# Second block's output projections: fp32 operands as they are, or split into two parts and multiplied in three passes

## The chip, the cores and the metric

The kernel runs on one core of a Trainium2 chip. Its time is the device time of one execution in microseconds (us), and a kernel's figure is the median over several executions. The engines named here are TensorE (PE, matrix products), VectorE (DVE), ScalarE (ACT), GpSimd (POOL) and SyncE (SP, which issues the loads). Each engine runs its instructions in the order in which they stand in its queue; semaphores make one engine wait for another.

## The reference, cut to what matters

The first part is a block of two layers (short convolution and retention) on 512 tokens of width 1024. Its result goes through a second block:

```
xn = rms_norm(h, norm1_g)
proj = xn @ w_in                      # queries, gates, values ...
o_hgrn = hgrn2_mixer(...)             # 4 heads of 128
o_gla  = gla_mixer(...)               # 4 heads of 128
mixed = concatenate([o_hgrn, o_gla])  # 512 tokens x 1024
h = h + mixed @ w_out                 # the output projections of the title
hn = rms_norm(h, norm2_g)
h = h + peer_ffn(hn, ...)             # top 16 of product keys, 128*128 experts
return rms_norm(h, norm_f_g)
```

All of it is in float32. `peer_ffn` computes queries `hn @ w_q`, compares them with sub-keys, and takes the top 16 of 8 heads twice. The kernel computes three of the four groups of 128 tokens densely over all experts, with a gate matrix made from the picks, and gathers the experts' rows for the fourth.

## The kernel before

A tensor is held with its 1024 columns on the partitions, in 8 pieces of 128, and its tokens along the free axis. The second block handles the tokens in two halves of 256. A weight matrix comes as tiles of 128 x 1024 through one list of tasks (`Weights`): SP loads the tiles in the list's order, and each task is then given its tiles.

A task can take its weights in two ways. With `direct=True` it gets the loaded tile, and `proj` (line 874) issues one fp32 matmul for each of the 8 pieces; the chip's profile shows each of them as two records. Otherwise ACT copies the tile to a tile `hi` of a shorter format (line 143), DVE subtracts it from the original and writes the rest to `lo` (line 151), and `proj` issues three matmuls for each piece: w hi by x hi, w hi by x lo, w lo by x hi (`PASSES`). The other operand has to be split as well, by `split_act` (lines 200 to 205) or `split_steps`: an ACT copy and a DVE subtraction. Splits of weights stand two tiles ahead of the task that uses them, with a raised priority.

The order of the second block is a list of words:

```
PLAN = "FQ00 P3 S00 P4 FQ01 S01 !N1 KG V0 G0 FQ10 S02 V1 S10 M00 FQ11 S11 G1 S12 M01 M10 O0 P8 M11 N0 Q00 O1 Q01 N1 P5 Q1"
```

The first digit is the half. S are the mixers' scores (line 1004 on PE, with DVE and ACT in between). M makes the mixer's outputs (`outs`, line 1124 on PE), their norm r (ACT, lines 214 to 1134), the normalised tiles `on` (DVE, line 1137), and transposes and gates them (`flips`, lines 1149 and 1151). O is the output projection: 8 tasks `wout_task` for each half, called at line 1541. Their input m is the gated tile itself. N is the norm behind it (x or hn), and Q the queries of the top 16 (`wq_task`), from half 0's split x (line 887) and half 1's fp32 hn (line 883). Keys are compared at line 1188. The selection of the top 16 (`top_k`, lines 1314 to 1385, mostly on DVE) and the gate matrices (`oh` on DVE, lines 1438 and 1445; products on PE, line 1453; copies on ACT, line 1462) are generators in the background: a few steps of them are issued at each tick, that is during and after each weight task. The expert products follow at lines 1718 and 1721 (up) and 1765 (down).

A scheduler that estimates durations orders the instructions on every engine when the program is built, with priorities from the order of issue. So an added instruction can move others.

Of the kernel before, what the change touches and what calls it, by code (L numbers as in the profile page):

```python
# [8 lines left out]
F32R = mybir.dt.float32r  # L9
# [14 lines left out]
HALF = 256  # L24
# [145 lines left out]
def tile_kernel(ctx: ExitStack, tc: tile.TileContext, ins, out):  # L170
# [15 lines left out]
    def ps_tile(role="a"):  # L186
        tag, n = psum["roles"].get(role, psum["roles"]["a"])
        return psum["pool"].tile([128, 512], F32, tag=tag, bufs=n, name="ps")
# [12 lines left out]
    def split_act(hl, src):  # L201

        x = nc.scalar.activation(hl[0], src, AF.Copy)
        nc.vector.tensor_tensor(out=hl[1], in0=src, in1=hl[0].bitcast(F32), op=OP.subtract)  # L204
        return x
# [87 lines left out]
    g = blocks.enter_context(tc.tile_pool(name="g", bufs=1, reuse_waits="tile"))  # L293
    NT = 10

    def slot(name, n=T, dt=F32):
        tag, bufs = SLOTS.get(name, ("g", NG))
        return g.tile([128, n], dt, tag=tag, bufs=bufs, name=name)
# [4 lines left out]
    def do(f, *a):  # L303
        W.add(lambda: f(*a))
# [530 lines left out]
    halves = []  # L835

    def second_block():
            def col(j):
                return cols2[:, j:j + 1]
# [30 lines left out]
            def pair(x):  # L870

                return x.rearrange("p (c t) -> p c t", c=2)
# [17 lines left out]
            def half(s):  # L890
                t0 = NM + HALF * s
                d = {}
# [250 lines left out]
                def flips(grp, i):  # L1143
                    p = ps_tile("o")
                    for hh in range(2):
                        h = 2 * i + hh
                        for t in range(2):
                            o = hh * HALF + t * 128
                            nc.tensor.transpose(p[:, o:o + 128], d["on", grp, t][:, h * 128:(h + 1) * 128], ident)
                    g = d.pop(("gate", grp, i))  # L1150
                    nc.vector.scalar_tensor_tensor(out=g, in0=p, scalar=col(E_HG + grp), in1=g, op0=OP.mult,
                                                   op1=OP.mult)
                    for hh in range(2):
                        d["m", 4 * grp + 2 * i + hh] = pair(g)[:, hh]
                    if i == 1:
                        for t in range(2):
                            d.pop(("on", grp, t))
# [60 lines left out]
            def pair_both(which, c):  # L1218

                def f(w):  # L1220
                    ds = [h["d"] for h in halves]
                    if c == 0:
                        for d in ds:
                            d["ps"] = ps_tile("ab")
                    proj(w, [(d["ps"][:, c * HALF:(c + 1) * HALF], d["x"]) for d in ds])
                    if c == 1:
                        for d in ds:
                            d[which, 2] = slot(which, 2 * HALF)
                            nc.scalar.activation(d[which, 2], d["ps"], AF.Copy, scale=0.125 if which == "q" else 1.0)
                return f  # L1230
# [35 lines left out]
            def v_task(grp, kp):  # L1266
                def f(w):
                    if kp == 0:
                        vps[:] = [(h["d"], t, ps_tile("v")) for h in halves for t in range(2)]
                    w = [x.rearrange("p (k c) -> p k c", c=512) for x in w]  # L1270
                    for kk in range(2):
                        k = 2 * kp + kk
                        for d, t, p in vps:
                            for n, (xi, wi) in enumerate(PASSES):
                                nc.tensor.matmul(p, d["x"][k][:, xi, t * 128:(t + 1) * 128], w[wi][:, kk, :],
                                                 start=(k == 0 and n == 0), stop=(k == KD - 1 and n == 2))
                    if kp == 3:
                        for j, (d, t, p) in enumerate(vps):
                            v = slot("v", 512)
                            nc.scalar.activation(v, p, AF.Copy)  # L1280
                            d["v", grp, t] = v
                            if j < 2:
                                first["v", grp, t] = v
                        vps.clear()
                return f

            def gate_task(grp, c):
                def f(w):
                    ds = [h["d"] for h in halves]
                    if c % 2 == 0:  # L1290
                        for d in ds:
                            d["ps"] = ps_tile("ab")
                    o = c % 2 * HALF
                    proj(w, [(d["ps"][:, o:o + HALF], d["x"]) for d in ds])
                    if c % 2:
                        for d in ds:
                            d["gate", grp, c // 2] = (slot if d is ds[1] else tb)("gate", 2 * HALF)
                            nc.scalar.activation(d["gate", grp, c // 2], d["ps"], AF.Silu)
                    if grp == 1 and c == 3:
                        for d in ds:  # L1300
                            d.pop("x")
                return f
# [180 lines left out]
            def add(f, direct=False, at=None):  # L1483
                W.add(f, n[0] if at is None else at, direct=direct)
                n[0] += at is None
# [4 lines left out]
            def back(s, f, *a, **k):  # L1490
                do(lambda: W.later(halves[s][f](*a), **k))
# [4 lines left out]
            def mixed(s, grp):  # L1496
                if s == 1:
                    for h in range(4):
                        call(s, "across", 4 * grp + h)
                        do(W.pump, 1)  # L1500
                call(s, "outs", grp)
                do(W.pump, 2)
                for i in range(2):
                    call(s, "flips", grp, i)
                    do(W.pump, 2)

            def retrieve(s, at, part=None):
                if part != 1:
                    call(s, "load_keys")
                for c in (range(16), range(QCUT), range(QCUT, 16))[0 if part is None else part + 1]:  # L1510
                    add(halves[s]["wq_task"](c), direct=s == 1, at=at + c)
                if part != 0:
                    call(s, "keys", 15)

            def step(name, *a):
                a = [int(x) for x in a]
                s = a[0] if a else 0
                if name == "FQ":
                    g2 = a[1]
                    for k, which in enumerate("fq"):  # L1520
                        for c in range(2):
                            add(halves[s]["pair_task"](which, 2 * g2 + c), direct=s == 0, at=N0 + 4 * g2 + 2 * k + c)
                elif name == "S":
                    back(s, "scores", a[1], name=f"S{s}{a[1]}")
                elif name == "KG":
                    for k, which in enumerate("kq"):
                        for c in range(2):
                            add(pair_both(which, c), at=N0 + 8 + 2 * k + c)
                    do(low_gate)
                elif name == "V":  # L1530
                    for kp in range(4):
                        add(v_task(s, kp), at=N0 + 12 + 8 * s + kp)
                elif name == "G":
                    for c in range(4):
                        add(gate_task(s, c), at=N0 + 16 + 8 * s + c)
                elif name == "M":
                    do(W.flush, *(f"S{s}{g}" for g in ((0, 1), (2,))[a[1]]))
                    mixed(*a)
                elif name == "O":
                    for m in range(KD):  # L1540
                        add(halves[s]["wout_task"](m), direct=True, at=N0 + 28 + m)
                elif name == "N":
                    back(s, "norm2", name="norm2", first=True)
                    do(W.flush, "norm2")
                elif name == "Q":
                    retrieve(s, N0 + 36, *a[1:])

            N0 = 256
# [3 lines left out]
            for word in PLAN.split():  # L1552
                if word[0] == "!":
                    do(W.flush, *word[1:].split(","))
                elif word[0] == "P":
                    pace(PACE[int(word[1:])])
                else:
                    name = word.rstrip("01234")
                    step(name, *word[len(name):])
# [401 lines left out]
```

## Time and profile before

| | us |
|---|---|
| median of 3 runs | 3293.77 (3293.57 to 3298.85) |
| the profiled execution | 3293.37 |
| its span on the core | 3291.6 |
| PE busy | 3250.3 (99%) |
| DVE busy | 2036.7 (62%) |
| ACT busy | 1302.2 (40%) |

The span goes from the first instruction to the last. A busy PE is one with a matmul in its pipe: a record's duration is longer than the distance to the next one, so the distance between starts is the price of one. The second block's output projections of half 0 run from 1885 to 1943 us, among the mixers' last steps, those of half 1 from 2010 to 2038, among the top-16 work. A row of the timeline merges neighbouring instructions of one kind.

### The profile page before, as it was taken

How to read it: one execution, taken by the hardware profiler on the slowest of the kernel's cores; microseconds unless marked ns; L12 is line 12 of the kernel's file. 1: busy time of each engine (PE TensorE's matmuls, PEld its weight loads, DVE VectorE, ACT ScalarE, POOL GpSimd, SP SyncE). 2: the span in 40 equal slices, each digit the busy share in tenths (PEclk: the TensorE clock that was granted, in tenths of full speed). 3: DMA queues.
4: the chain of work that ended last, by engine and by line, in shares of the span. 5: the costliest groups of instructions: out<-in, count | busy, mean ns of one | idle time of the engine just before them, and what ended most of it. 6: DMA issues, size and time to landing. Idle time of an engine off the chain costs nothing. (4 is left out here: it accounts for less than half of the span.)

```text
span 3291.6 us, 51099 instructions
## 1 busy us (share of the span) xinstructions
PE 3250.3 (99%) x21063; PEld 2974.2 (90%) x21063; DVE 2036.7 (62%) x4019; ACT 1302.2 (40%) x2388; POOL 186.3 (6%) x132
## 2 busy tenths in 40 slices
PE   8999999999999999999999999999999999999999
PEld 7999999999889999999998988766789999999998
DVE  6545554433744555443465659998898888888443
ACT  5343242323534324232455533356443333333333
POOL 0000000000000000000000000000132222222000
PEclk9999999999999999999999999999999999999999
DMA  6222222222422222222232123346899988998442
GB/s 216 75 86 88 77 78 90 90 90 103 176 75 99 87 84 78 90 90 100 106 129 90 52 91 140 129 181 239 305 373 346 345 333 314 351 356 325 143 147 95
DMA packets 129961, 532.04 MB, mean 162 GB/s; under 512 B 9136, under 2 KB 60992, under 8 KB 73280
## 3 DMA queue, kind: packets, MB, share of 16 engines
q1 hardware_dynamic: 103520, 368.19, 31.2%
q0 software_dynamic: 18432, 134.23, 10.6%
q10 hardware_dynamic: 7776, 26.37, 2.0%
q8 instruction: 165, 2.70, 0.3%
q14 instruction: 68, 0.56, 0.0%
HBM read 501.48 MB, written 27.26 MB: 161 GB/s over the span
## 5 line engine op out<-in xcount | busy, mean ns | idle before, releaser
L143 ACT ACTIVATE hi<-raw 128x1024 fp32r<-128x1024 f32 x532 | 563.4, 1060 | 1404.1 <-PE ps L386 626.7
L151 DVE TENSOR_TENSOR lo<-raw,hi 128x1024 fp32r<-128x1024 f32 x532 | 650.6, 1224 | 753.3 <-ACT hi L143 748.4
L386 PE MATMUL ps<-xnh,hi 128*128 128x256 f32 (+1 forms) x2464 | 513.7, 283 | 0.0
L386 PE MATMUL ps<-xnl,hi 128*128 128x256 f32 (+1 forms) x2464 | 513.5, 283 | 0.0
L386 PE MATMUL ps<-xnh,lo 128*128 128x256 f32 (+1 forms) x2464 | 512.9, 283 | 0.0
L1765 PE MATMUL ps<-hi,hw 128*128 128x512 f32 x1536 | 427.0, 393 | 3.3 <-ACT hid L1730 2.8
L1721 PE MATMUL ps<-hn,hi 128*128 128x384 f32 x1600 | 409.5, 337 | 0.0
L386 PEld LDWEIGHTS ps<-xnh,lo 128*128 128x128 f32 x2464 | 385.8, 189 | 0.0
L386 PEld LDWEIGHTS ps<-xnh,hi 128*128 128x128 f32 x2464 | 384.7, 188 | 1.1
L386 PEld LDWEIGHTS ps<-xnl,hi 128*128 128x128 f32 x2464 | 384.4, 188 | 0.1
L1635 POOL DMA_INDIRECT uv<-uv,idx x128 | 186.1, 1454 | 2843.8 <-PE ps L1650 2336.8
L1765 PEld LDWEIGHTS ps<-hi,hw 128*128 128x128 f32 x1536 | 287.7, 188 | 63.6 <-ACT hid L1730 3.5
L1721 PEld LDWEIGHTS ps<-hn,hi 128*128 128x128 f32 x1600 | 290.8, 188 | 4.3
L1721 PE MATMUL ps<-hn,lo 128*128 128x384 f32 x800 | 269.2, 337 | 0.0
L1765 PE MATMUL ps<-lo,hw 128*128 128x512 f32 x768 | 239.5, 392 | 0.0
L1765 PEld LDWEIGHTS ps<-lo,hw 128*128 128x128 f32 x768 | 144.7, 188 | 32.1
L1663 DVE SCALAR_TENSOR_TENSOR acc<-uv,dots,acc 128x1024 f32<-128x1024 f32 x127 | 163.0, 1284 | 3.2
L1671 DVE SCALAR_TENSOR_TENSOR uv<-uv,hnT 128x1024 f32<-128x1024 f32 x128 | 155.8, 1219 | 10.5 <-DMA uv<-uv,idx 10.4
L1718 PE MATMUL ps<-hn,raw 128*128 128x384 f32 x448 | 149.5, 490 | 5.0 <-ACT stage L1462 4.7
L1721 PEld LDWEIGHTS ps<-hn,lo 128*128 128x128 f32 x800 | 150.0, 188 | 0.1
L887 PE MATMUL ps<-x,hi 128*128 128x256 f32 x768 | 141.4, 288 | 4.0 <-ACT x L274 3.4
L1718 PEld LDWEIGHTS ps<-hn,raw 128*128 128x128 f32 x448 | 83.4, 190 | 62.6 <-ACT stage L1462 8.1
(353 smaller groups left out, 5103.6 us busy)
## 6 DMA issues: line engine op xcount, KB each, us to landing
raw<-ws SPq DMA_DIRECT2D x313, 1024.0 KB, 4.8
gate_d<-stage ACTq DMA_DIRECT2D x48, 512.0 KB, 3.4
gates<-gate_d SPq DMA_DIRECT2D x16, 1536.0 KB, 13.1
dm<-decay_m SPq DMA_DIRECT2D x8, 264.0 KB, 5.1
vb<-vbias SPq DMA_DIRECT2D x8, 256.0 KB, 6.3
dc<-decay SPq DMA_DIRECT2D x8, 256.0 KB, 5.6
uv<-uv,idx POOLq DMA_INDIRECT x128, 7.6
h<-ht SPq DMA_DIRECT2D x2, 544.0 KB, 4.4
```

The source lines that it names most:

```text
L143: nc.scalar.activation(hi, raw[i], AF.Copy)
L151: nc.vector.tensor_tensor(out=lo, in0=r, in1=parts[i][0].bitcast(F32), op=OP.subtract)
L386: nc.tensor.matmul(t[:, :b - a], w[wi][:, off + k, :], x[k].t[xi][:, a:b], start=(k == 0 and n == 0), stop=(k == K - 1 and n == 2))
L887: nc.tensor.matmul(p, parts[wi][:, k, :], x[k][:, xi], start=(k == 0 and n == 0), stop=(k == K - 1 and n == 2))
L1635: nc.gpsimd.indirect_dma_start(out=t, out_offset=None, in_=ins["uv"], in_offset=bass.IndirectOffsetOnAxis(ap=idx[i][:, j:j + 1], axis=0))
L1663: nc.vector.scalar_tensor_tensor(out=acc, in0=v, scalar=dots[:, j:j + 1], in1=acc, op0=OP.mult, op1=OP.add)
L1671: nc.vector.scalar_tensor_tensor(out=u, in0=u, scalar=1.0, in1=hnT, op0=OP.mult, op1=OP.mult, accum_out=dots[:, j:j + 1])
L1718: nc.tensor.matmul(ps, w[0][:, k, :], tl["hn32"][k][:, :ND], start=k == 0, stop=k == KD - 1)
L1721: nc.tensor.matmul(ps, w[wi][:, k, :], tl["hn"][k][:, xi], start=(k == 0 and n == 0), stop=(k == KD - 1 and n == 2))
L1765: mm = nc.tensor.matmul(tl["acc"][t][b], h[:, hi, t * 128:(t + 1) * 128], w[vi][:, b * 512:(b + 1) * 512], start=(e == 0 and n == 0), stop ...
```

## The change

The eight tasks of each half no longer take their weights directly, and each m is split when it is made: `flips` copies each half of the gated tile to a new tile (hi) and subtracts it (lo). The new tiles come from the same ring of 43 slots (`slot`) as the other tiles of the block.

```diff
                     for hh in range(2):
-                        d["m", 4 * grp + 2 * i + hh] = pair(g)[:, hh]
+                        x = d["m", 4 * grp + 2 * i + hh] = pair(slot("m", 2 * HALF, F32R))
+                        split_act([x[:, 0], x[:, 1]], pair(g)[:, hh])
...
                     for m in range(KD):
-                        add(halves[s]["wout_task"](m), direct=True, at=N0 + 28 + m)
+                        add(halves[s]["wout_task"](m), at=N0 + 28 + m)
```

In the changed file every line after 1154 has a number that is one higher.

The orders of SP and POOL are the same in both. Those of PE, DVE and ACT differ at many places; here are three. The first is DVE while half 0's output projections run, before the change: the gated tiles (L1151), then the scores of the next heads (L1013, L973, L1033), and the sum of an output projection into h (L1164).

```order
L1151 SCALAR_TENSOR_TENSOR gate<-ps,cols_91,gate 128x512 x2
L1065 TENSOR_TENSOR qe<-qe,pr 128x2x128
L1013 TENSOR_TENSOR P<-ps,masks 128x512
L1164 TENSOR_TENSOR h<-ps,h 128x256
L1013 TENSOR_TENSOR P<-ps,masks 128x512
L973 TENSOR_TENSOR e<-cum 128x512 x4
L1033 TENSOR_TENSOR ke<-cum 128x512
```

The same place with the change (from the gated tiles on; L204 is the subtraction that makes the lo part of m):

```order
L1151 SCALAR_TENSOR_TENSOR gate<-ps,cols_91,gate 128x512 x2
L973 TENSOR_TENSOR e<-cum 128x512
L204 TENSOR_TENSOR m<-gate,m 128x256 x2
L1018 COPY_PREDICATED P<-masks,ps 128x8x32
L1065 TENSOR_TENSOR ke<-ke,el 128x2x64
L1065 TENSOR_TENSOR qe<-qe,el 128x2x64 x2
L986 TENSOR_TENSOR e<-e,q 128x128x2
L986 TENSOR_TENSOR e<-e,k 128x128x2
L1018 COPY_PREDICATED P<-masks,ps 128x4x64
L1065 TENSOR_TENSOR qe<-qe,pr 128x2x128
L1013 TENSOR_TENSOR P<-ps,masks 128x512 x2
L973 TENSOR_TENSOR e<-cum 128x512 x4
```

Then come L1033 and the other two L204. The first output projection's sum into h has moved behind them. The PE order around it has m products, with the scores' products between them.

The second place is ACT just before the first query projection of half 0. Before, from the mixers' last squares (L1129, with a table load and r) to the copies of x:

```order
L1129 ACTIVATE so,ms<-ps 128x128 x8
L214 ACT_TABLE_LOAD
L216 ACTIVATE r_19371<-ms,eps_66 128x8
L1134 ACTIVATE r_19371<-r_19371 128x8
L274 ACTIVATE x<-nt 128x256 x8
```

With the change:

```order
L1129 ACTIVATE so,ms<-ps 128x128 x8
L214 ACT_TABLE_LOAD
L216 ACTIVATE r_19567<-ms,eps_66 128x8
L1134 ACTIVATE r_19567<-r_19567 128x8
L203 ACTIVATE m<-gate 128x256 x4
L274 ACTIVATE x<-nt 128x256 x8
```

Four copies of m, for half 1's projections, now stand between r and x. On PE, the eight transposes that lead to them stand ahead of the first x product, where three x products came first before; on DVE, both gate products and four L204 stand ahead of the lo parts of x.

The third place is DVE while half 1's output projections run, amid the top-16 work. Before:

```order
L1164 TENSOR_TENSOR h<-ps,h 128x256
L1322 MAX top<-sc 128x8
L1356 TENSOR_SCALAR m<-pos 128x32
L1346 TENSOR_TENSOR cand<-top 128x2x32
L1346 TENSOR_TENSOR cand<-top 128x2x48
L1346 TENSOR_TENSOR cand<-top 128x2x8
L1322 MAX top<-sc 128x8
```

With the change (in this file the sum into h is L1165, and the subtraction of a weight is L151):

```order
L1165 TENSOR_TENSOR h<-ps,h 128x256
L1357 TENSOR_SCALAR m<-pos 128x32
L1347 TENSOR_TENSOR cand<-top 128x2x32
L151 TENSOR_TENSOR lo<-raw,hi 128x1024
L1347 TENSOR_TENSOR cand<-top 128x2x48
L1347 TENSOR_TENSOR cand<-top 128x2x8
L1360 TENSOR_SCALAR m_20532<-pf 128x32
```

From the first top-16 instruction (L1314) to the thirteenth L1438 of the gate matrices, DVE's order has 16 L151 where it had 8; all other counts in that piece are the same.

## Rows read from the trace of the kernel before

**Rows 1.** The page's table of engines: busy us, share, instructions.
```profile
PE 3250.3 (99%) x21063; PEld 2974.2 (90%) x21063; DVE 2036.7 (62%) x4019; ACT 1302.2 (40%) x2388; POOL 186.3 (6%) x132
```
**Rows 2.** Stretches: us; PE, PEld, DVE, ACT, POOL busy (instructions); PE clock; DMA share, GB/s.
```profile
1885.00:1945.00 60.00, 59.66 (x390) 51.83 (x388) 33.84 (x72) 22.46 (x64) 0.00 (x0) 1.00 0.21 72
1945.00:1958.00 13.00, 9.33 (x66) 7.96 (x66) 3.37 (x9) 8.15 (x27) 0.00 (x0) 0.99 0.43 157
1960.00:1970.00 10.00, 10.00 (x70) 10.00 (x68) 4.90 (x10) 2.96 (x5) 0.00 (x0) 0.78 0.04 7
1980.00:2158.00 178.00, 173.10 (x913) 143.89 (x913) 172.61 (x996) 63.81 (x162) 0.00 (x0) 0.98 0.35 125
2326.00:3291.00 965.00, 958.26 (x4768) 861.14 (x4768) 721.30 (x1031) 356.61 (x612) 186.09 (x128) 1.00 0.77 286
```
**Rows 3.** Line 883: operation, count, duration ns (min/median/max), first and last start.
```profile
L883 PE MATMUL ps<-gate,raw x256: 377/379/483, 1885.0 to 2038.3; 128*128 128x256 f32 x128
```
**Rows 4.** Timeline of PE (start, length, operation); last row: line 887's busy time.
```profile
1935.83 1.10 PE L1004 MATMUL ps<-qe,ke 64*128 64x64 f32 x8
1936.86 5.45 PE L883 MATMUL ps<-gate,raw 128*128 128x256 f32 x24
1942.23 0.72 PE L1078 MATMUL ps<-qe,ke 64*128 64x128 f32 x8
...
1965.20:1970.10 4.90, 4.90 (x43) 4.87 (x42) 1.00 0.11 17
```
**Rows 5.** Timeline of DVE from the gated tiles to the scores of the next heads.
```profile
1893.94 1.41 DVE L1151 SCALAR_TENSOR_TENSOR gate<-ps,cols,gate 128x512 f32<-128x512 f32 x2 [1.52 <-PE ps L1149]
...
1901.94 0.69 DVE L1013 TENSOR_TENSOR P<-ps,masks 128x512 f32<-128x512 f32 x1 [0.66 <-PE ps L1004]
1902.55 2.49 DVE L973 TENSOR_TENSOR e<-cum 128x512 f32<-128x512 f32 x4
1904.95 0.69 DVE L1033 TENSOR_TENSOR ke<-cum 128x512 f32<-128x512 f32 x1
```
**Rows 6.** Timeline of all engines before half 0's first query projection.
```profile
1957.76 2.55 ACT L274 ACTIVATE x<-nt 128x256 fp32r<-128x256 f32 x8
1957.88 1.29 DVE L1137 TENSOR_TENSOR on<-ps,r 128x512 f32<-128x512 f32 x2 [6.25 <-ACT r L1134]
...
1958.21 1.01 PE L887 MATMUL ps<-x,hi 128*128 128x256 f32 x3 [3.39 <-ACT x L274]
...
1959.02 1.97 PE L1149 MATMUL ps<-ident,on 128*128 128x128 f32 x8
1959.09 2.09 DVE L271 TENSOR_TENSOR x<-nt,x 128x256 fp32r<-128x256 f32 x6
```
**Rows 7.** Timeline of DVE at its first top-16 instructions.
```profile
1978.78 1.23 DVE L151 TENSOR_TENSOR lo<-raw,hi 128x1024 fp32r<-128x1024 f32 x1 [2.05 <-ACT hi L143]
1979.92 1.64 DVE L1314 MAX8 top<-sc 128x8 f32<-128x128 f32 x8
...
1983.73 1.21 DVE L151 TENSOR_TENSOR lo<-raw,hi 128x1024 fp32r<-128x1024 f32 x1
1984.85 0.09 DVE L1319 MATCH_VALUE_LOAD sc<-top,sc 128x8 f32 x1
```
**Rows 8.** Waits of DVE, 1980.1 to 2158: us in total, times, longest.
```profile
DVE top L1314 <- ACT sc L1200: 2.7, 1, 2.7
DVE eq L1378 <- ACT eq L1375: 1.1, 1, 1.1
DVE rank L1370 <- ACT pos L1366: 0.7, 2, 0.4
```
**Rows 9.** Timeline of PE and DVE where the gate matrices begin.
```profile
2159.47 0.63 PE L1453 MATMUL ps<-oh 128*128 128x128 f16 x8 [0.18 <-DVE oh L1438]
...
2161.26 0.63 PE L1453 MATMUL ps<-oh 128*128 128x128 f16 x8 [0.26 <-DVE oh L1445]
...
2159.94 1.29 DVE L1445 TENSOR_TENSOR oh<-oh,picks 128x1024 f16<-128x1024 f16 x2
```

## The prediction

> **What bounds the kernel now.** I read the page's table of engines first. PE is busy for 99% of the span and DVE for 62% [rows 1], so on the average anything taken from PE should come back as time. The average hides a change of limits, so the second view was busy time by stretch [rows 2]. From 1885 to 1945 us, where the first half's output projections run, PE is full (59.66 of 60 us) and DVE a little over half busy: PE sets the pace. From 1945 to 1958 PE waits for a chain of small operations. From 1980 to 2158 both are full, PE 173.1 and DVE 172.6 of 178 us: DVE selects the top 16 keys there while PE computes queries, the second half's output projections and the first expert products. After 2326 PE alone is.
>
> So the question is what DVE's position is at 2158, when PE turns to gate-matrix products that read what DVE makes. The third view, the timeline there, says it: PE starts a product at 2159.47 after 0.18 us of waiting for DVE's oh, and another at 2161.26, when DVE's pair of L1445 (1.29 us from 2159.94) has just ended [rows 9]. PE is ahead by nothing: a DVE that comes later by more than some 0.3 us makes PE later.
>
> **First half, matmuls.** Removed: 8 tasks of 8 full fp32 products. The trace shows 256 records for both halves, two per product [rows 3], so 128 a half. A group of 24 starts at 1936.86 and the next work at 1942.23: 5.37/24 = 0.224 us each, 28.6 us a half [rows 4]. Added: 24 products a task, 192 a half, of the 256-column kind that the query projections use: 4.90 us hold 42 weight loads of them, 0.117 us each, 22.4 us [rows 4]. PE saves 28.6 - 22.4 = **6.2 us a half**. The Trainium skill (FP8 and Floating Point Precision, TensorE Precision Notes) counts a true fp32 product as four passes of the array, of which the change keeps three. By it alone the saving is an estimate of a quarter of 28.6, 7.2 us, and the sum below would be 1.0 us lower; the rows have 0.351 against 0.448 us, because a 256-column pass takes 0.117 us whatever its kind.
>
> **First half, operands.** Each weight tile now needs an ACT copy (hi) and a DVE subtraction (lo), each m a smaller pair. In 1885 to 1945 ACT (22.5 of 60 us) and DVE (33.8) have room for them [rows 2], so their work is free; their place in the queues is not. In DVE's new order the last two m remainders of this half stand behind two L1013, four L973 and one L1033. Once PE has done the eight q,k products that release L1013, DVE needs about 1.3 us for these two, 2.4 for four L973, 0.6 for L1033 [rows 5] and 0.7 for the two remainders (L271's spacing, 2.09 us for 6 [rows 6]): 5.0 us. PE has eight small e products in that time (16 records at 1.03/8 us, 2.1 us), three first-pass m products (0.35) and four L1100 (8 records; 1.0 at the same spacing) [rows 4]: 3.4 us. The difference is 1.6, with the hand-overs between the engines **2 us** of stall. Bounds: 0 if DVE is not behind, 6 if lo subtractions (1.12 us) push the scores' chain back as well.
>
> **The gap before the first query projection.** Before, r is ready when DVE starts on at 1957.88 and ACT has begun to copy x; PE starts at 1958.21, 0.33 us later [rows 6]. In the new ACT order four m copies (for the second half) come before the eight x copies. They wait for both normalised tiles (1.29 us on DVE), the eight transposes (1959.02 to 1960.99, so 1.8 us after DVE's end), a gate product (1.41 us for two, 0.7 for the second) and then take 0.6 us; the first x copy is 0.3 more [rows 5, 6]. That is 4.7 instead of 0.33 us: **+4.4 us**, from 3.5 (transposes at the spacing of a full clock) to 5. Nothing hides it: PE has no other work here, and 16 query tasks and all of the top-16 work stand behind it. First half together: -6.2 + 2 + 4.4 = +0.2 us, and DVE's first top-16 instruction, at 1979.92 before [rows 7], moves by the same.
>
> **Second half.** The 6.2 us that PE saves here lie inside 1980 to 2158. DVE has to do eight more lo subtractions in the same stretch: one starts at 1983.73 and the next instruction at 1984.85 [rows 7], so 8 x 1.12 = 9.0 us more in a queue that runs in order. What DVE can get back is its waiting, 4.5 us in three places [rows 8]. The longest wait, 2.7 us for a score that PE and ACT deliver, should go, since DVE comes to it later and PE earlier; so should the 1.1 us. The short ones are round trips and stay. **+9.0 - 3.8 = +5.2 us** at 2158; bounds 4.5 (all of it recovered) and 9.0 (none). PE's saving turns into waiting: it is early at the end of the output projections, waits for the normalised h that DVE makes in its turn, and waits again at 2159. Subtract the 0.3 us that it waited already [rows 9].
>
> **The clock.** After 3.39 us of idle PE before 1958.21 [rows 6] the granted clock from 1960 to 1970 was 0.78, a mixture of the two levels, 1.2 and 2.4 GHz [rows 2]. The new waits at 2159 come in two pieces, for a total of some 5 us. If the clock falls, the next records run at half speed for a few us; bounds 0 and 3 us (what 0.78 leaves out, 10 x 0.22 = 2.2, and a second fall in part). I take **+1**. The Trainium skill (TensorE: Matmul & The Clock Gate, HAM oscillation) says that a matmul stream that keeps waiting drops to the lower level again and again and pays each time. By that rule a kernel that gives PE less to do while others are late pays twice; the row of 0.78 agrees, and here it would mean the upper end, 3 us.
>
> **Nothing else.** The weights come by the same DMAs in the same order on SP and POOL, and gate_d's stores on ACT keep their places among the copies. The sixteen m tiles take slots of a ring of 43, and a wait for one is within the bound of 6 us above. Sum: +0.2 + 5.2 - 0.3 + 1 = **+6.1 us**. The profiled execution took 3293.4 us (span 3291.6), which gives 3299.5; the median of the runs shown is 0.4 higher, so **3300 us**. Behind the gate matrices nothing is changed and PE is busy for 958 of 965 us [rows 2], so no later stage gives it back.
>
> **Rivals.** *PE stays the bound (faster).* If DVE's selection work has slack that the timeline does not show, or if the scores reach it early enough for it to start well before, both savings count: -12.4 + 2 + 4.4 = -6 us, 3287, or 3285 without the stall. For it: PE's 173.1 us is no less than DVE's 172.6 in that stretch [rows 2]. Against it: 0.18 and 0.26 us of waiting for DVE at its end [rows 9], and only 4.5 us of waiting in 178 on DVE. It decides if DVE reaches 2158 by its own order before PE does. Chance 0.12. *The two halves cancel.* No stall and a gap at its lower end give -6.2 + 3.5 = -2.7, DVE +4.5, no clock loss: +1.5, about 3295. Chance 0.18; the forecast with its own spread, +2 to +9, has 0.46. *More waits than these (slower still).* The longer DVE and ACT queues hold up the scores' chain at several points (stall 6), lo waits for hi behind top-16 copies on ACT, and nothing is recovered: -6.2 + 6 + 4.4 + 9.0 + 1 = +14, 3308. For it: before the top-16 stage DVE already waited 2.05 us for an ACT hi ahead of one lo [rows 7]. Against it: ACT is busy for 64 of 178 us there. Chance 0.24.
>
> **The numbers.** A difference under 0.2%, 6.6 us, is about what measurement can't tell from none. Faster by more needs most of the first rival: 0.08. Slower by more (over 3300.4) is all of the last rival and nearly half of the forecast's spread: 0.24 + 0.21 = 0.45. Within: 0.47. The range leaves out the lower part of the first rival and the top of the last one: 3288 to 3309.
>
> **What would show it.** Right: two records per product gone from the projections, 192 three-pass products at 0.117 us; PE waiting longer than 3.4 us before the first query product, with ACT's four m copies ahead of x; DVE full from 1980 on with eight more L151; PE waits at the first gate products that grow from 0.2 to several us, released by DVE's oh. Wrong: a first gate product that comes earlier than before, or DVE idle in that stretch by more than 5 us. The forecast fails if DVE's gate operands are ready when PE arrives.

## The result, and the profile after

The changed kernel takes 3316.93 us (median of 6 runs, 3314.29 to 3320.09), the kernel before beside it 3293.67 (6 runs): ratio 1.007, interval 1.0059 to 1.0080. It is 23 us slower. The forecast was 3300 with a range up to 3309: slower was its tilt, the size is wrong.

First the page's table of engines after the change, which answers to [rows 1]:

```profile
PE 3252.9 (98%) x21191; PEld 2979.9 (90%) x21191; DVE 2058.9 (62%) x4051; ACT 1322.2 (40%) x2421; POOL 184.9 (6%) x132
```

The sums hardly moved. The stretches do; columns as in [rows 2], the first two and the fourth at the same times as there:

```profile
1885.00:1945.00 60.00, 53.65 (x369) 50.61 (x368) 43.39 (x88) 34.00 (x91) 0.00 (x0) 0.86 0.11 38
1945.00:1958.00 13.00, 13.00 (x116) 12.21 (x114) 8.68 (x19) 5.16 (x10) 0.00 (x0) 1.00 0.26 87
...
1980.00:2158.00 178.00, 169.44 (x1045) 148.34 (x1044) 166.13 (x858) 70.46 (x160) 0.00 (x0) 0.97 0.37 131
```

In the stretch where PE was full (59.66 of 60) it now stands for 6.35 us, at a granted clock of 0.86 where it was 1.00. Cut finer, from 1880 on:

```profile
1880.00:1890.00 10.00, 6.67 (x55) 6.27 (x53) 7.67 (x12) 8.02 (x22) 0.00 (x0) 1.00 0.26 106
1890.00:1900.00 10.00, 5.53 (x31) 5.39 (x31) 4.73 (x13) 9.91 (x21) 0.00 (x0) 0.79 0.00 0
1900.00:1910.00 10.00, 10.00 (x48) 9.81 (x47) 8.78 (x20) 3.05 (x10) 0.00 (x0) 0.50 0.01 2
1910.00:1920.00 10.00, 9.77 (x64) 8.76 (x64) 4.99 (x13) 3.59 (x10) 0.00 (x0) 0.86 0.00 0
```

Read the clock column downwards: after two slices with PE busy for 6.7 and 5.5 us it is 0.50, the lower of the two levels (1.2 GHz), for a whole slice in which PE is busy all the time. So an idle PE was paid twice. What it waited for, from 1880 to 1982 (us in total, times, longest):

```profile
PE ps L1149 <- DVE on L1137: 4.1, 2, 3.8
PE ps L887 <- ACT gate L1299: 3.3, 1, 3.3
PE ps L1004 <- DVE P L1018: 2.8, 1, 2.8
PE ps L887 <- ACT x L274: 1.9, 1, 1.9
PE ps L1004 <- ACT q L935: 1.7, 1, 1.7
PE ps L1100 <- ACT PA L1103: 1.5, 1, 1.5
```

The second, third and fifth row, 7.8 us, lie before the first across product (L1100) and have no counterpart before. Two of them are scores' products (L1004); the 3.3 us stand before a product of the output projection itself (L887, with m), which waits for an ACT step. All three lie in one stretch in which ACT hardly pauses (fourth group of numbers, 19.35 of 19.5 us):

```profile
1882.00:1901.50 19.50, 11.71 (x75) 11.05 (x73) 12.67 (x27) 19.35 (x46) 0.00 (x0) 0.85 0.13 54
```

Six of these ACT steps are loads of a function table (ACT_TABLE_LOAD, 1.28 us each), and the DVE step of the third row stands behind one that waited 3.46 us for ACT's e (L976). So PE stands in the end for ACT. A full ACT alone does not stop it: before, ACT is busy for 14.60 of the 15.20 us from 1874.90 on, and PE for all of them. What has changed is which steps come together there.

Why they do, the timeline of DVE some 35 us earlier begins to tell, at the first scores of half 1. After the change:

```profile
1851.04 0.69 DVE L973 TENSOR_TENSOR e<-cum 128x512 f32<-128x512 f32 x1 [1.81 <-PE ps L1004]
...
1859.43 1.23 DVE L151 TENSOR_TENSOR lo<-raw,hi 128x1024 fp32r<-128x1024 f32 x1 [0.93 <-ACT hi L143]
1865.06 1.22 DVE L151 TENSOR_TENSOR lo<-raw,hi 128x1024 fp32r<-128x1024 f32 x1 [4.40 <-ACT hi L143]
1866.38 1.90 DVE L973 TENSOR_TENSOR e<-cum 128x512 f32<-128x512 f32 x3
```

Before:

```profile
1846.52 0.68 DVE L973 TENSOR_TENSOR e<-cum 128x512 f32<-128x512 f32 x1
...
1848.25 0.68 DVE L973 TENSOR_TENSOR e<-cum 128x512 f32<-128x512 f32 x1
...
1850.04 0.73 DVE L973 TENSOR_TENSOR e<-cum 128x512 f32<-128x512 f32 x1
...
1851.01 0.69 DVE L973 TENSOR_TENSOR e<-cum 128x512 f32<-128x512 f32 x1
```

Each L973 makes a new tile e, a slot of the ring of 43. Before, four of them come within 4.5 us and DVE waits for none of them; after, one, and the next 15 us later, though DVE is idle for much of that time. L973 reads only cum, which DVE made itself, so the 1.81 us for which the first one waits for PE can only be a wait for the place of its output: PE's products have to be done with an older tile there. The chain of scores has been put off, and what PE did in place of it (other weight tasks) it lacks 30 us later.

All runs are compared at the same events below: starts of the first rows of such kind on PE, for the top 16 on DVE, in us. "q,k" is the first score product of the next heads (L1004 with q and k, 128 x 128), "gap" the distance from the start of the last row of output products (v by PA) to the first query product, "gates" the distance from the first to the last row of gate products. Runs differ by up to 1.7 us already at 1843, where the order is still the same (L1065's product with pr: 1843.24 in E4, 1843.45 before, 1844.95 after).

| run | q,k | first across | gap | first top-16 | gates | median us | ratio (95%) |
|---|---|---|---|---|---|---|---|
| before | 1870.0 | 1897.1 | 4.45 | 1979.9 | 152.0 | | |
| after | 1884.3 | 1910.0 | 8.89 | 1996.9 | 157.9 | 3316.9 | 1.0070 (1.0059 to 1.0080) |
| E1 m in the ring | 1883.8 | 1912.2 | 6.88 | 2000.0 | 152.0 | 3313.9 | 1.0057 (1.0043 to 1.0071) |
| E2 half 1 only | 1871.4 | 1898.5 | 9.13 | 1983.6 | 157.3 | 3306.6 | 1.0036 (1.0022 to 1.0049) |
| E3 half 0 only | 1884.0 | 1909.7 | 4.45 | 1992.7 | 152.3 | 3305.5 | 1.0031 (1.0019 to 1.0043) |
| E4 parked | 1870.9 | 1895.0 | 9.13 | 1980.5 | 158.1 | 3301.7 | 1.0017 (1.0008 to 1.0026) |
| E5 half 0 parked | 1871.8 | 1895.9 | 4.46 | 1977.0 | 153.8 | 3290.5 | 0.9989 (0.9981 to 0.9998) |
| E6 DVE load | 1870.2 | 1897.4 | 4.46 | 1978.7 | 153.7 | 3300.7 | 1.0017 (1.0008 to 1.0026) |
| E7 one slot | 1877.5 | 1898.5 | 4.46 | 1983.4 | 152.5 | 3295.5 | 1.0005 (0.9997 to 1.0014) |
| E8 GpSimd, deferred | 1871.6 | 1895.7 | 4.45 | 1978.6 | 153.2 | 3300.0 | 1.0014 (1.0006 to 1.0023) |
| E9 half 1, no w lo | 1870.3 | 1897.5 | 9.13 | 1987.0 | 152.2 | 3296.5 | 1.0004 (0.9995 to 1.0013) |
| E10 parked, deferred | 1871.3 | 1895.4 | 4.45 | 1977.8 | 158.2 | 3295.8 | 1.0007 (0.9998 to 1.0016) |
| E11 half 0 parked, 44 | 1872.1 | 1894.9 | 4.45 | 1976.5 | 152.6 | 3290.6 | 0.9988 (0.9979 to 0.9997) |
| E12 half 0's m in the ring | 1882.8 | 1909.2 | 4.45 | 1994.4 | 151.6 | 3311.1 | 1.0049 (1.0035 to 1.0063) |

The kernel before had medians of 3295.7 beside E1 to E4, 3294.8 beside E5 to E8 and 3294.1 beside E9 to E12.

### The profile page after: what moved, and what is told of

Its sections match the earlier page's. It is cut to its first block, busy times and chain, and to the rows that moved or that the text cites. A ratio compares the mean times of both kernels' runs of the same rounds, so it can differ in the third digit from the quotient of the medians.

```text
span 3316.0 us, 51452 instructions
## 1 busy us (share of the span) xinstructions
PE 3252.9 (98%) x21191; PEld 2979.9 (90%) x21191; DVE 2058.9 (62%) x4051; ACT 1322.2 (40%) x2421; POOL 184.9 (6%) x132
## 4 chain that ended last, share of the span: by engine, by line
PE 89%; DVE 6%; ACT 3%; DMA 1%; issue 1%; DVEq 0%; ACTq 0%; SPq 0%
PE ps L386 37%; PE ps L1766 15%; PE ps L1722 13%; PE ps L454 5%; PE ps L887 4%; PE ps L1719 3%; PE ps L1004 2%; PE ps L549 2%; PE ps L688 2%; PE ps L396 1%; PE ps L1276 1%; PE ps L498 1%; ACT stage L1463 1%; PE ps L450 1%; DMA gates<-gate_d 1%; DVE lo L151 1%
## 5 line engine op out<-in xcount | busy, mean ns | idle before, releaser
L143 ACT ACTIVATE hi<-raw 128x1024 fp32r<-128x1024 f32 x548 | 580.2, 1060 | 1421.0 <-PE ps L386 627.1
L151 DVE TENSOR_TENSOR lo<-raw,hi 128x1024 fp32r<-128x1024 f32 x548 | 671.0, 1225 | 759.9 <-ACT hi L143 757.8
L887 PE MATMUL ps<-x,hi 128*128 128x256 f32 x768 | 139.4, 287 | 2.7 <-ACT x L274 1.9
```

The costliest lines, as they stand in the source:

```text
L143: nc.scalar.activation(hi, raw[i], AF.Copy)
L151: nc.vector.tensor_tensor(out=lo, in0=r, in1=parts[i][0].bitcast(F32), op=OP.subtract)
L887: nc.tensor.matmul(p, parts[wi][:, k, :], x[k][:, xi], start=(k == 0 and n == 0), stop=(k == K - 1 and n == 2))
```

## The experiments

**Theory R (ring).** `slot` hands out 43 buffers to the whole block. Half 0's gate tiles, in which its m lay before, are not among them: they come from `tb`, the ring of 10 for nt, so and on (`(slot if d is ds[1] else tb)("gate", 2 * HALF)`). The change gives half 0 eight slots, from the flips to the end of its output projections. The next half's scores take theirs from the same 43 and get them later. **Theory Q (queues)**, its rival: the copies and subtractions of the splits stand in the queues of ACT and DVE ahead of the chain.

E1 leaves the splits out and takes the slots (the diff; each gate product becomes two); E12 does so for half 0 alone, E7 for half 0 with one product and one slot a flip in place of two:

```diff
-                    nc.vector.scalar_tensor_tensor(out=g, in0=p, scalar=col(E_HG + grp), in1=g, op0=OP.mult,
-                                                   op1=OP.mult)
                     for hh in range(2):
-                        d["m", 4 * grp + 2 * i + hh] = pair(g)[:, hh]
+                        x = d["m", 4 * grp + 2 * i + hh] = slot("m", 2 * HALF)[:, :HALF]
+                        nc.vector.scalar_tensor_tensor(out=x, in0=pair(p)[:, hh], scalar=col(E_HG + grp),
+                                                       in1=pair(g)[:, hh], op0=OP.mult, op1=OP.mult)
```

> The kernel before, with one thing of the change: each m is written by its gate product to a slot of its own of the 43-slot ring (two products of 256 columns a flip in place of one of 512), where half 0's m lay in the ring of nt/so/on tiles before. No split, projections in fp32 as before, and the result is the same. Theory R (ring): the eight m slots of half 0 are what pushes the next half's score chain back; the q,k products that start at 1870 us before and at 1884 after start at 1880 or later here too, PE stands still for 4 us or more before the first across product, and the time is 3302 to 3312. Theory Q (queues: the split copies and subtractions on ACT and DVE hold the chain up): nothing of it here, 3292 to 3296.

> The kernel before, fp32 projections, no split; only half 0's gate products are written, in two products of 256 columns a flip, to eight slots of the 43-slot ring; half 1's stay in place. Theory R: eight slots of half 0 alone make the loss of the run where both halves' m had slots of their own (3313.9), q,k products at 1882 to 1886, 3306 to 3314. If half 1's slots made part of it: 3298 to 3305.

> The kernel before, half 0's gate products written to one slot of the 43-slot ring for each flip (four slots in all, where the run with eight for half 0 and eight for half 1 took 18 us), everything else as before. Theory R with a dose: a smaller shift of the q,k products (they stand 33 PE records later than before in the order, where eight slots put them 79 later), 1872 to 1880 us, and 3297 to 3307. If only the half-1 tiles or the split in two products matter: 3294 to 3297.

E1 lost 18 us with the arithmetic of the kernel before. E12's waits of PE from 1860 to 1985 have the changed kernel's three (the second row is the gap, as long as before):

```profile
PE ps L1004 <- DVE P L1018: 4.5, 1, 4.5
PE ps L887 <- ACT x L274: 3.4, 1, 3.4
PE ps L883 <- ACT gate L1298: 2.6, 1, 2.6
PE ps L1004 <- ACT q L935: 1.7, 1, 1.7
```

8.8 us in the first, third and fourth row, against 7.8. Here the second e waits in plain sight, on DVE:

```profile
1865.27 1.90 DVE L973 TENSOR_TENSOR e<-cum 128x512 f32<-128x512 f32 x3 [6.22 <-PE ps L1124]
```

L1124 are the output products, which read the score tiles P, slots of the same ring. They run at 1862.85 in E12 and at 1863.95 in the changed kernel, just ahead of this second e, and at 1881.43 before. Eight slots cost 17 us (3311.1 against 3294.1), the q,k products come 12.8 us late; half 1's slots add some 1 us at most (18 in E1). With four slots (E7) they come 7.5 us late, yet the time, for which I expected 3297 or more, is no different from before: the shift has a dose, but only the larger one cost time. Theory Q can't explain any of it, since no operand is split here. E7's time is also what I expected if the cut of each gate product in two made the loss; E3 and E5 below, which leave these products whole, decide against that.

E4 is the reverse: all of the change, but half 0's m off the ring. The lo parts go to the ring of 10, four hi parts to buffers that hold something else earlier or later, four to two slots:

```diff
+                        if s == 0:
+                            if hh == 0:
+                                lo = pair(tb("mlo", 2 * HALF).bitcast(F32R))
+                            x = d["m", 4 * grp + 2 * i + hh] = [parked(4 * grp + 2 * i + hh), lo[:, hh]]
+                            split_act(x, pair(g)[:, hh])
+                            continue
...
+            def parked(k):
+                if k < 4:
+                    return hp.tile([128, HALF], F32R, tag=("glp", "picks0", "picks1", "picks2")[k], bufs=1, name="mhi")
+                if k % 2 == 0:
+                    first["park"] = slot("m", 2 * HALF, F32R)
+                return pair(first["park"])[:, k % 2]
```

> The full change with the same number of splits and passes, but half 0's m tiles taken off the 43-slot ring: four hi parts in buffers that hold other things at other times (the low-rank gate's weights before, the picks after), four in two slots, the lo parts in the ring of nt/so/on tiles. Six slots fewer are held than in the changed kernel. Theory R: the q,k products start within 3 us of 1870, PE waits less than 3 us before the first across product, half 0 is 0 to 6 us faster than before at its end, and the time is 3297 to 3306 (the second half's loss of 5 to 8 us stays). Theory Q: the ACT and DVE work is the same, 3314 to 3319.

3301.7, 6.0 us over its before. The slice that stood at clock 0.50, and PE's waits from 1860 to 1985:

```profile
1900.00:1910.00 10.00, 9.88 (x73) 8.60 (x71) 8.01 (x17) 4.38 (x12) 0.00 (x0) 1.00 0.01 2
```

```profile
PE ps L1157 <- DVE on L1145: 4.8, 3, 3.8
PE ps L895 <- ACT x L274: 1.9, 1, 1.9
PE ps L1108 <- ACT PA L1111: 0.8, 1, 0.8
PE ps L1012 <- DVE P L1026: 0.3, 1, 0.3
```

The waits ahead of the first across product are gone (0.3 is left); the gap before the first query, 4.8 + 1.9, is still there.

**The halves apart.** E2 and E3 do the change for one half (`direct=s != 1` and `direct=s != 0`, with m the gated tile in the other); E5 is E3 with E4's parking; E11 is E5 with `NG = 44`.

> The change for half 1 alone; half 0's weights direct and its m the gated tile as before. Theory R and theory Q both put the 12.8 us that the trace after has lost by the first across product (1897.1 against 1909.9) into half 0: here that product starts within 1 us of 1897 plus the 1.5 us by which the whole trace after is later. What is left is the gap ahead of the first query (+2 to +4.4) and the eight lo subtractions in the top-16 work (+4.9): 3299 to 3304. If the loss came from somewhere else (the half-1 tiles, code or placement common to both), 3308 or more.

> The change for half 0 alone; half 1 direct. Theories R and Q: the loss of about 13 us by the first across product is here in full, and no gap of four m copies ahead of x and no extra subtractions in the top-16 work: the first top-16 instruction 12 to 15 us late, the end 3304 to 3310. If the two halves only lose together: under 3300.

> Half 0 alone in three passes, its m tiles off the 43-slot ring as in the run with parked tiles; half 1 direct as before. Theory R: no chain pushed back, no four copies ahead of x, no extra subtractions in the top-16 work. The chain of the last scores ended 7 us earlier in the parked run, the last across and output products 2.4 us earlier, so 2 to 4 us come back: 3289 to 3294. If PE's 6.2 us come back in full: 3286 to 3289. If the extra splits cost what the passes save: 3294 to 3298.

> Half 0 alone in three passes with parked m (3290.5), and one slot more in the ring (44, all that the memory leaves). Theory R: the parked kernel still holds two slots more than before, its q,k products start 1.8 us later than before's; one slot gives back at most that: 3288 to 3291. If the ring no longer matters there: 3289 to 3292, the same within what can be told apart. The scheduler's order can shift by chance: over 3293 would be that.

E3: +9.8 us against its before, with the q,k and across products as late as after the change; E5: -4.3. They differ only in the place of m (and in the buffers that E5 borrows for it): 14 us. E5 beats both kernels (interval of the ratio under 1), by little; one more slot (E11) adds nothing. E2: +10.9 us, half 0 as expected (first across at 1898.5), but more in all than the 3299 to 3304 expected.

**What half 1 pays with.** E6 puts only its DVE load into the kernel before; E9 takes only that load out of E2 (its weights' lo part is left out of the computation, and PE multiplies hi a second time in its place).

```diff
+                        if s == 1:          # E6, in wout_task
+                            lo = W.pool.tile([128, 1024], F32, tag="lo", bufs=SUBS_AHEAD + 1, name="lo")
+                            nc.vector.tensor_tensor(out=lo, in0=w, in1=w, op=OP.subtract)
...
+                if flat[i][1] == "hi":      # E9, in Weights.run; half 1's tasks have direct="hi"
+                    parts[i] *= 2
```

> The kernel before with eight DVE subtractions of 128x1024 fp32 into the lo ring, one in each of half 1's output projections, their results unused: DVE's share of the change in half 1 by itself, without weight copies on ACT, without split m, with the fp32 products. Theory D (DVE bounds the top-16 stretch): 9.0 us more on DVE less at most 4.5 us of recovered waits put the gate products 4.5 to 9 us later, 3298 to 3305, and the first long wait of PE is at the first gate products. If DVE has slack there: 3294 to 3297, and the half-1 loss of 5 us lies with ACT or with the passes.

> The change for half 1 alone, but its weights' lo part is left out of the computation: the third pass multiplies hi a second time, so PE, ACT's weight copies and the split m stay as in the run with half 1 alone (3306.6), and only the eight DVE subtractions of 128x1024 are gone. Theory D (DVE is what half 1 pays with): DVE reaches the gate products 5 to 9 us earlier than in that run, PE's 3.9 us wait there falls under 1.5, 3297 to 3302. If the loss lies with the copies on ACT or with the first query alone: 3304 to 3308.

E6: +5.9 us (interval 2.6 to 8.6); its profiled execution was its fastest, at 3293.8, so its gates in the table say little. E9: +2.4 us against its before where E2 had +10.9, so 8.5 us went with the subtractions, against the 5.9 that they cost alone, although the gap of 9.13 us is still there; its profiled execution was its slowest, at 3301.3. Its waits of PE from 2150 to 2190 have nothing over 0.7:

```profile
PE ps L1459 <- ACT stage L1468: 1.6, 5, 0.6
PE ps L1724 <- ACT stage L1468: 1.6, 3, 0.7
PE ps L1459 <- DVE oh L1444: 0.5, 2, 0.3
```

In the changed kernel the wait stands here, where [rows 9] had 0.26 us; PE in the first gate products, and ACT:

```profile
2174.91 0.62 PE L1454 MATMUL ps<-oh 128*128 128x128 f16 x8 [0.24 <-ACT stage L1463]
2179.48 1.01 PE L1454 MATMUL ps<-oh 128*128 128x128 f16 x8 [3.94 <-ACT hid L1731]
```

```profile
2177.30 0.23 ACT L1367 ACTIVATE pos<-f 128x32 uint32<-128x32 f32 x1 [2.44 <-DVE f L1366]
2178.59 0.23 ACT L1356 ACTIVATE pf<-pos 128x32 f32<-128x32 uint32 x1 [1.06 <-DVE pos L1325]
...
2178.96 0.47 ACT L1731 ACTIVATE hid<-ps 128x384 f32<-128x384 f32 x1
```

PE waits for a buffer that ACT empties (L1731). ACT was not busy: its queue stood at two small steps of the top 16 that wait for DVE. DVE's lateness reaches PE through the queue of a third engine.

**Repairs.** E10 is E4 with the last four m splits of half 1 issued behind the x splits; E8 has, besides, half 1's weight subtractions on GpSimd:

```diff
-                        split_act([x[:, 0], x[:, 1]], pair(g)[:, hh])
+                        (behind.append if grp else lambda a: split_act(*a))(([x[:, 0], x[:, 1]], pair(g)[:, hh]))
...
                     do(W.flush, "norm2")
+                    if s == 0:
+                        do(lambda: [split_act(*a) for a in behind])
```

> The full change, half 0's m off the ring, the last four m splits of half 1 issued behind the x splits, weight subtractions on DVE. Against the parked run (3301.7, first query 9.1 us after the last output product) the first query comes 4.4 to 4.7 us after it, as before; at the first top-16 instruction 2.3 us are left of that, since the early query products lose less to the half clock: 3298 to 3301. If those 4.5 us are on the path in full: 3296 to 3298. If DVE takes them again at the gate products: 3301 to 3304.

> The full change with three repairs: half 0's m off the ring; the last four m splits of half 1 issued behind the x splits; half 1's eight weight subtractions on GpSimd, which has nothing to do there. Theories R and D: the first query starts 0 to 1 us after r as before, DVE reaches the gate products 0 to 3 us later than before for the m splits alone, PE's wait there is under 3 us: 3286 to 3296. If a GpSimd subtraction of 128x1024 takes so long that PE waits for lo, or slows DVE beside it: 3298 or more, with PE waiting for lo in the second output projections.

E10 is 1.7 us over its before, not to be told from it, where E4 was 6.0 over its own; its time is under all three expected. The gap is back at 4.45. But at the gate products, which PE reaches 2.65 us earlier than before (2146.95 against 2149.60), it waits longer than ever:

```profile
2155.50 0.63 PE L1469 MATMUL ps<-oh 128*128 128x128 f16 x8 [0.24 <-ACT stage L1478]
2161.71 3.75 PE L1469 MATMUL ps<-oh 128*128 128x128 f16 x32 [5.58 <-ACT hid L1748]
```

So what PE has gained by then it loses in this wait. E8 missed (3298 or more was expected if PE had to wait for lo; the long waits are others): a GpSimd subtraction takes 2.40 us where DVE takes 1.22, the gate wait shrank (153.2), but half 1's hn came 7.2 us later than before (2053.99 against 2046.76), and PE waited 3.8 us for DVE's sum into h on the way. What of that is GpSimd's length and what a DVE put in another order was not separated.

## Why the prediction was wrong

The step that failed is one sentence: the sixteen m tiles "take slots of a ring of 43, and a wait for one is within the bound of 6 us above". It costed the new tiles at nothing beyond a stall, without asking where the old ones lived. Half 0's eight were new to the ring. Their price was 17 us (E12; 17 between the changed kernel and E4, each against its own before; 14 between E3 and E5), about the 17 us by which the result lies above the forecast, and its place was not the stall of 2 us that I put behind L973 and L1033 but a chain put off 30 us earlier, in a stretch (1843 to 1885) that I took as unchanged. I read the new order from the output projections on; the first place at which it differs from the old one is before them.

**The other steps held.** *First half, matmuls and operands:* -6.2 + 2 = -4.2 us forecast; with m off the ring -4.3 (E5; interval -6.3 to -0.7). That the two figures meet is in part luck: the interval holds -6.2 too, so no run shows the 2 us of stall or the place that the prediction gave it. Nor do the rows bear out its reason for 0.351 against 0.448 us: four passes of 0.117 would be 0.468, and a quarter of 0.448 is 0.112; the sum does not need it. *The gap:* 4.7 instead of 0.33, +4.4 forecast; 8.89 instead of 4.45 measured, +4.4, with the four m copies ahead of x (they answer to the L274 of [rows 6], which began before L1137):

```profile
1975.41 1.58 ACT L203 ACTIVATE m<-gate 128x256 fp32r<-128x256 f32 x4 [2.87 <-DVE gate L1151]
1976.89 2.24 ACT L274 ACTIVATE x<-nt 128x256 fp32r<-128x256 f32 x7
```

Not all of it reached the end of the stretch (1979.9 to 1983.6 in E2, of which 1.4 was there at 1870), but moving the copies gave 4.3 us back (6.0 in E4, 1.7 in E10, each against its own before). *Second half:* +5.2 - 0.3 and a part of the clock's +1; the gates took 157.9 us instead of 152.0, +5.9. The recovered waits were as read from [rows 8]: from 1997 to 2175 DVE waited 1.4 us, where it had 4.7 (the 4.5 of [rows 8] and 0.2 for sm); 3.3 us came back, 3.8 were forecast:

```profile
DVE eq L1379 <- ACT eq L1376: 0.8, 1, 0.8
DVE rank L1371 <- ACT pos L1367: 0.4, 1, 0.4
DVE sm L1407 <- ACT gwt L1405: 0.2, 1, 0.2
```

One detail was wrong: I expected oh (L1438) as the releaser. It was ACT's copy behind two steps that wait for DVE. Half 1 as a whole: 4.4 + 5.2 - 0.3 + 1 = 10.3 forecast, +10.9 in E2 (interval 7 to 16). *The sum:* +6.1 without the ring; E4, which is the change without most of the ring's load, has +6.0 (interval 2.6 to 8.6).

**The clock** was mis-sized in the first half: bounds of 0 and 3 us for the whole change. From 1890 to 1920 alone 10 x (0.21 + 0.50 + 0.14) = 8.5 us are missing from the full clock, part of it while PE stood. Parking the tiles removed it with the waits (1.00 in each of the three slices of E4). From 1970 to 1980, where the gap ends, it is 0.71, and behind the wait at the gates 0.71 again (2180 to 2190). That is the Trainium skill's warning about a stream that keeps waiting (TensorE: Matmul & The Clock Gate, HAM oscillation); the trace agrees with these three falls, and the prediction put it only into the second half.

**The rivals.** *PE stays the bound* fell: E10's PE comes early and waits. *More waits* (3308) had the sign and too little of the size, with the wrong mechanism: DVE recovered its waits, and the queues by themselves cost nothing in half 0 (E5).

**Open** stays why the scheduler put the output products ahead of the late e and the other steps where they are: the order is made when the program is built, and the traces show only its outcome and the waits for slots in it (1.81 us after; 1.93 and 6.22 in E12). That ACT's table loads are what makes the chain's delay dear is read from the trace and not tested. Nor did I divide the 12.9 us by which the first across product is late between the 7.8 us of waits, the half clock and the saved passes.

## What to carry to other kernels

Before a new tile is costed at nothing, look up which ring the tile it replaces lived in, who else draws on the new one, and from when to when it is held; then read the scheduler's order from where the tile is made, not from where it is used. Work on a half-empty engine is free only until a queue that runs in order puts it ahead of somebody's next step: four copies of 0.4 us cost some 4. And taking work from a full engine pays only where the next engine isn't full: of two equal halves one gave 4 us, the other lost 11.

## What the runs showed of the hardware that was not expected

The clock is at 0.50 for a full slice of 10 us in which PE is busy throughout (1900 to 1910), behind 20 us with PE busy for 12.2: much of the cost comes when the waits are over.

Recorded lengths can grow without any loss of time. The MATCH_REPLACE8 of sc (128 x 128; L1319 before, L1320 after) between 1980 and 2170 had a mean length of 0.284 us before and 0.337 after, but the next instruction mostly started 0.19 us behind it in both. For these short DVE instructions the distance between starts is the price, not the length.
